# Deferred sum splits, a fifth pair of split weights, and seven products that grow in two PSUM tiles

## The chip, the cores and the metric

One core of one Trainium2 chip runs the whole program. The time is the device time of one execution in microseconds (us). TensorE (PE) multiplies, VectorE (DVE), ScalarE (ACT) and GpSimd (POOL) work elementwise, and SyncE (SP) issues the loads. Each engine works through its own list of instructions in the order in which the program was written or scheduled; an instruction that waits for another engine holds up all behind it.

## The reference

One step of a decoder layer over 1024 prompt tokens and 8 × 4 sample tokens, model width 1024. A mixing layer (windowed attention beside trailing-mean pooling) is followed by the part that this change touches, a feed-forward layer with 2816 hidden channels, and by an input per layer:

```python
f = _rms(x, n_ffn_pre)
f = (jax.nn.silu(f @ w_gate) * (f @ w_up)) @ w_down
x = x + _rms(f, n_ffn_post)
x = x + jax.nn.sigmoid(x @ w_ple_gate) * (p @ w_ple)
```

All is float32, to float32's accuracy.

## The kernel before

**Split products.** A float32 operand is split by `split` into a high part, cast on ACT (L164), and a low part, the rest, subtracted on DVE (L165). A product is three matmuls: high × high, high × low, low × high. All matmuls are issued from line 126; the tokens are the moving operand, 352 at a time, since the 1056 tokens form three groups `g` of 352.

**Weights.** Raw weights of 512 KB are loaded by SP into `wr` (`W_RAW` buffers), and split into `wh` and `wl` (`W_PAIRS` pairs, which also hold the sums `sh`, `sl`). `need(k)` makes all items up to `LOOK` = 4 ahead of the one wanted, in the order of `ITEMS`.

**Seven products.** For token groups 0 and 1 the gate and up product of one chunk of 128 channels is made with seven half-sized products instead of eight. The gate weight `wg` and the up weight `wu` give P1 and P2 and T4 (`p4`) by their quarters; four more products, S1 to S4, use sums and differences of quarters of both. POOL makes these in place in the raw buffers with four instructions (`w_sums`, L990), and then ACT and DVE split the two results into `sh` and `sl`. The token side (`B11`, `T1` and so on) was made once before. Each product (12 matmuls) has a PSUM tile of its own (`bank`, eight in turn); DVE adds them up from there (L1024), silu of the gate part is on ACT (L1036, L1067), and the two products of gate and up, one for each of the two token groups, go into `hid` with a split of their own (`hid_put`). Group 2 is multiplied directly (24 matmuls for gate, 24 for up).

**The walk.** There are 11 slabs of two chunks. `WALK` takes slabs 0 to 4 for group 2 alone (while other work still runs), slabs 5 to 10 for all three groups, and slabs 0 to 4 again for groups 0 and 1. The last five are called slabs 1 to 5 in what follows. In each, for chunk pair i = 0: P1, P2, then `pending()`, which is the down products of the slab before (six matmuls for each of 8 columns and each group; the high and low parts of `hid` for two chunks; DVE adds the result into `o`, L1087), then p4, S2, S3, S1, S4. "The downs of slab 2" are those that run inside slab 2. For pair i = 1 there are no downs: p4 and the S products follow P1 and P2. In the slabs with group 2, p4 stands between S3 and S1.

**Beside it.** When group 2 is finished (downs of slab 1), `ple_steps` follow in pieces: the norm factor is spread over the partitions by small matmuls, DVE multiplies `o` with it from a PSUM tile (L1115) and adds it to `x` (L1119).

Of the kernel before, what the change touches and what calls it, by code (L numbers as in the profile page):

```python
# [12 lines left out]
AF = mybir.ActivationFunctionType  # L13
ALU = mybir.AluOpType
# [33 lines left out]
UEXT = PST + DSEQ  # L48
ULEN = UPRE + SEQ + NDEC * UEXT

W_PAIRS = 4
W_RAW = 3


WARM = 8
# [6 lines left out]
def trunk_kernel(  # L62
# [31 lines left out]
    nc = tc.nc  # L94
    te, ve, se, ge = nc.tensor, nc.vector, nc.scalar, nc.gpsimd
# [28 lines left out]
    def mm(*args, **kw):  # L124

        ins = te.matmul(*args, **kw)  # L126
# [36 lines left out]
    def split(hi, lo, src):  # L163
        fix(se.copy(hi, src))  # L164
        fix(ve.tensor_tensor(lo, src, hi.bitcast(F32), op=ALU.subtract))  # L165
# [3 lines left out]
    def w_load(j):  # L169
        if j >= len(plan) or j in raws:  # L170
            return
        src, shape = plan[j]
        t = wpool.tile(shape, F32, tag="wr", bufs=W_RAW, name=nm("wr"))
        nc.sync.dma_start(t, src)
        raws[j] = t

    def w_tile(shape, s):
        return wpool.tile(shape, F32R, tag="wp", bufs=2 * W_PAIRS, name=nm(s))

    def w_split(j):  # L180
        if j >= len(plan) or j in pairs:
            return
        w_load(j)
        shape = plan[j][1]
        hi, lo = w_tile(shape, "wh"), w_tile(shape, "wl")
        split(hi, lo, raws[j])
        pairs[j] = (hi, lo)

    lazy = [False]

    def weights(j, ahead=W_PAIRS - 1):
        for i in range(j, j + (0 if lazy[0] else ahead) + 1):
            w_split(i)
            w_load(i + 1)
        return pairs[j]
# [19 lines left out]
    WALK += [(s, (0, 1)) for s in range(AHEAD)]  # L215
    ITEMS = []

    def item(kind, *js):
        ITEMS.append((kind, js))
        return len(ITEMS) - 1  # L220

    def direct_item(src, shape):
        return item("direct", add_plan(src, shape))

    WGU, WD = [], []
    for s, gs in WALK:
        pairs_of = []
        for i in range(SLAB):
            c = SLAB * s + i
            jg = direct_item(w_gu[c, 0], [P, KC, P])  # L230
            if 0 not in gs:
                ju = direct_item(w_gu[c, 1], [P, KC, P])
            if i == 0 and WD:
                last_s = WALK[len(WD) - 1][0]
                WD[-1] = [direct_item(w_dn[last_s, j], [P, SLAB, 512]) for j in range(2)]
            if 0 in gs:
                ju = direct_item(w_gu[c, 1], [P, KC, P])
            js = item("sums", jg, ju) if 0 in gs else None
            pairs_of.append((jg, ju, js))
        WGU.append(pairs_of)  # L240
        WD.append(None)
# [20 lines left out]
    made = {}  # L262

    def need(k, ahead=LOOK):

        for i in range(len(made), min(k + ahead + 1, len(ITEMS))):
            kind, js = ITEMS[i]
            if kind == "direct":
                w_split(js[0])
                made[i] = pairs[js[0]]  # L270
            else:
                made[i] = w_sums(*(raws[ITEMS[j][1][0]] for j in js))
            for kind, js in ITEMS[i + 1 : i + 3]:
                if kind == "direct":
                    w_load(js[0])
        return made[k]

    def gemm(ps, ops, start=True, stop=True):

        last = len(ops) - 1  # L280
        for i, (wh, wl, xh, xl) in enumerate(ops):
            mm(ps, wh, xh, start=start and i == 0, stop=False)
            mm(ps, wh, xl, start=False, stop=False)
            mm(ps, wl, xh, start=False, stop=stop and i == last)

    def ops8(w, xs):

# [53 lines left out]
    def load(dst, src):  # L341
        tc.keep_in_program_order(nc.sync.dma_start(dst, src))  # L342
# [92 lines left out]
    n = 4 * NDEC * PST  # L435
# [145 lines left out]
    for c in range(4):  # L581
        n = NDEC * DSEQ
# [356 lines left out]
    f7 = {}  # L939
# [37 lines left out]
    def hid_put(g, slot, ht):  # L977
        split(new_hid[g][:, slot, :], new_hid[g][:, SLAB + slot, :], ht)

    def w_sums(a1, a2):  # L980


        a11, a12, a21, a22 = a1[:, 0:4, :], a1[:, 4:8, :], a2[:, 0:4, :], a2[:, 4:8, :]
        for out, a, b, op in (
            (a22, a21, a22, ALU.add),
            (a21, a11, a21, ALU.subtract),
            (a11, a22, a11, ALU.subtract),
            (a12, a12, a11, ALU.subtract),
        ):
            ge.tensor_tensor(out, a, b, op=op)  # L990
        two = []
        for src in (a1, a2):
# [4 lines left out]
        return {"S2": quarter(s24, 0), "S4": quarter(s24, 1), "S3": quarter(s31, 0), "S1": quarter(s31, 1)}  # L997

    def ops4(w, x):

        return [(w[0][:, k, :], w[1][:, k, :], x[0][:, k, :], x[1][:, k, :]) for k in range(4)]

    def quarter(w, h):
        return tuple(t[:, 4 * h : 4 * h + 4, :] for t in w)

    def gate_up(items, slot, gs, pending):

        ig, iu, is_ = items
        n = N

        def product(w, x):
            ps = bank()
            gemm(ps[:, :n], ops4(w, x))
# [9 lines left out]
        def add(out, a, ps):  # L1023
            ve.tensor_tensor(out, a, ps, op=ALU.add)  # L1024

        wg = need(ig)
        if 0 in gs:
            p1 = tmp(n, "p1")
            se.copy(p1, product(quarter(wg, 0), f7["B11"]))
        if 2 in gs:  # L1030
            sl = tmp(n, "sl")
            se.activation(sl, direct(wg), AF.Silu)
        if 0 in gs:
            c11 = tmp(n, "c11")
            add(c11, p1, product(quarter(wg, 1), f7["B21"]))
# [4 lines left out]
        if 2 in gs:  # L1040
            ve.tensor_tensor(sl, sl, direct(wu), op=ALU.mult)
        for g in gs:
            if slot == 0:
                new_hid[g] = half(g, F32R, "hid")
        if 2 in gs:
            hid_put(2, slot, sl)
        if pending and 0 not in gs:
            pending()
        if 0 not in gs:
            return  # L1050
        if 2 not in gs:
            p4 = product(quarter(wu, 1), f7["T4"])
        s = need(is_)
        add(p1, p1, product(s["S2"], f7["T2"]))
        u3 = tmp(n, "u3")
        add(u3, p1, product(s["S3"], f7["T3"]))
        c21 = tmp(n, "c21")
        if 2 in gs:
            p4 = product(quarter(wu, 1), f7["T4"])
        add(c21, u3, p4)  # L1060
        ve.tensor_tensor(c21, c21, c11, op=ALU.mult)
        hid_put(0, slot, c21)
        p5 = product(s["S1"], f7["T1"])
        add(u3, u3, p5)
        add(p1, p1, p5)
        add(p1, p1, product(s["S4"], f7["B22"]))
        se.activation(p1, p1, AF.Silu)  # L1067
        ve.tensor_tensor(u3, u3, p1, op=ALU.mult)
        hid_put(1, slot, u3)

    os_ = [None] * G

# [204 lines left out]
```

## Time and profile before

| what | value |
|---|---|
| time, median of 3 runs | 1118.11 us (1117.52 to 1119.99) |
| the profiled execution, its own time | 1118.37 us |
| its span, first to last instruction | 1116.6 us |
| mean granted TensorE clock | 0.998 |
| busy, ACT | 440.0 us, 39% |
| DMA moved | 99.54 MB, 89 GB/s |

The span is that of the instructions; the execution is 1.8 us longer. Times in the timelines count from the span's start. The feed-forward part runs from about 219 to 1112 us.

### The profile page before, as it was taken

Reading aid. Unit: us, or ns where it says so; the run is one execution under the profiler, and the core shown is the slowest. Engines: PE = TensorE matmul, PEld = TensorE weight load, DVE = VectorE, ACT = ScalarE, POOL = GpSimd, SP = SyncE. Lnnn points to the kernel's source line nnn. Section 1 sums busy time; section 2 is a strip of 40 time slices with the busy share of each in tenths; the row PEclk is TensorE's granted clock in tenths of the full one; section 3 lists DMA queues with packets and bytes.
Section 4 is the critical chain, followed back from the end, with each engine's and each line's share of the span. In section 5 each row is a group of like instructions: output and inputs, shape, how many; then the busy total and the mean of one; then the engine's idle time right before and its main releaser. Section 6 shows DMA issues by size and latency. Waiting matters only on the chain.

```text
span 1116.6 us, 17703 instructions
## 1 busy us (share of the span) xinstructions
PE 1106.5 (99%) x7171; PEld 1089.6 (98%) x7171; DVE 748.3 (67%) x1241; ACT 440.0 (39%) x779; POOL 179.4 (16%) x152
## 2 busy tenths in 40 slices
PE   8999999999999999999999999999999999999998
PEld 8999988899999999999999999999999999999998
DVE  6667478886979955255564555547887877789532
ACT  8323276664645523331222313123424334365220
POOL 0045032200000131011111102112132123100000
PEclk9999999999999999999999999999999999999999
DMA  8121311542543212121120202122112222336211
GB/s 289 56 71 38 122 43 38 194 157 85 203 166 129 99 38 76 39 76 39 38 60 17 78 36 76 38 100 79 57 58 83 70 76 80 124 133 222 85 58 39
DMA packets 35217, 99.54 MB, mean 89 GB/s; under 512 B 4132, under 2 KB 14660, under 8 KB 35136
## 3 DMA queue, kind: packets, MB, share of 16 engines
q1 hardware_dynamic: 33808, 96.65, 25.5%
q10 hardware_dynamic: 1328, 1.77, 0.5%
q8 instruction: 56, 0.92, 0.3%
q14 instruction: 25, 0.20, 0.1%
HBM read 88.30 MB, written 10.11 MB: 88 GB/s over the span
## 4 chain that ended last, share of the span: by engine, by line
PE 93%; DVE 3%; DMA 1%; issue 1%; POOL 1%; ACT 1%; SPq 0%; DVEq 0%; POOLq 0%
PE b L126 92%; PE b L120 1%; DMA xr<-in_x_dram 1%; DVE wl L165 1%; POOL wr L990 0%; SPq L342 0%; DVE h L368 0%; DVE o L1115 0%; DVE x L1119 0%; DVE mx L628 0%; DVE a L736 0%; DVE p L1024 0%; DVE hid L165 0%; ACT h L366 0%; ACT xr L377 0%
## 5 line engine op out<-in xcount | busy, mean ns | idle before, releaser
L126 PE MATMUL b<-fh,wh 128*128 128x352 f32 x808 | 260.7, 323 | 0.0
L126 PE MATMUL b<-fh,wl 128*128 128x352 f32 x808 | 259.3, 321 | 0.0
L126 PE MATMUL b<-fl,wh 128*128 128x352 f32 x808 | 259.0, 321 | 0.0
L126 PE MATMUL b<-hid,wh 128*128 128x352 f32 x1056 | 252.5, 322 | 1.8 <-DVE o L1115 1.2
L164 ACT CAST wh<-wr 128x1024 fp32r<-128x1024 f32 (+1 forms) x139 | 143.0, 1031 | 248.9 <-PE b L126 205.6
L165 DVE TENSOR_TENSOR wl<-wr,wh 128x1024 fp32r<-128x1024 f32 (+1 forms) x139 | 170.5, 1229 | 57.9 <-ACT wh L164 53.9
L126 PEld LDWEIGHTS b<-hid,wh 128*128 128x128 f32 x1056 | 182.3, 188 | 2.6 <-issue 1.5
L126 PE MATMUL b<-hid,wl 128*128 128x352 f32 x528 | 169.0, 320 | 0.0
L990 POOL TENSOR_TENSOR wr<-wr 128x512 f32<-128x512 f32 x44 | 63.4, 1441 | 623.0 <-DVE wl L165 621.3
L126 PEld LDWEIGHTS b<-fl,wh 128*128 128x128 f32 x808 | 151.9, 188 | 0.0
L126 PEld LDWEIGHTS b<-fh,wl 128*128 128x128 f32 x808 | 151.8, 188 | 0.0
L126 PEld LDWEIGHTS b<-fh,wh 128*128 128x128 f32 x808 | 151.6, 188 | 0.0
L1087 DVE TENSOR_TENSOR o<-o,b 128x352 f32<-128x352 f32 x240 | 114.9, 516 | 29.3 <-PE b L126 29.3
L126 PE MATMUL b<-fh,sh 128*128 128x352 f32 x352 | 113.6, 323 | 0.0
L126 PE MATMUL b<-fl,sh 128*128 128x352 f32 x352 | 112.7, 320 | 0.0
L126 PE MATMUL b<-fh,sl 128*128 128x352 f32 x352 | 112.7, 320 | 0.0
L126 PE MATMUL b<-h,wh 128*128 128x352 f32 x480 | 105.5, 325 | 0.9 <-ACT h L366 0.6
L165 DVE TENSOR_TENSOR sl<-wr,sh 128x1024 fp32r<-128x1024 f32 x44 | 53.8, 1222 | 75.5 <-ACT sh L164 75.5
L126 PEld LDWEIGHTS b<-hid,wl 128*128 128x128 f32 x528 | 98.9, 187 | 0.0
L164 ACT CAST sh<-wr 128x1024 fp32r<-128x1024 f32 x44 | 45.7, 1047 | 130.9 <-POOL wr L990 91.2
L126 PEld LDWEIGHTS b<-h,wh 128*128 128x128 f32 x480 | 81.9, 189 | 2.2 <-DVE h L368 1.2
L126 PE MATMUL b<-h,wl 128*128 128x352 f32 x240 | 66.3, 326 | 0.0
(150 smaller groups left out, 1591.0 us busy)
## 6 DMA issues: line engine op xcount, KB each, us to landing
wr<-in_w_gu_dram SPq DMA_DIRECT2D x64, 512.0 KB, 3.3
wr<-in_w_dn_dram SPq DMA_DIRECT2D x32, 512.0 KB, 3.3
wr<-in_w_pg_dram SPq DMA_DIRECT2D x14, 512.0 KB, 3.6
x<-in_x_dram SPq DMA_DIRECT2D x6, 704.0 KB, 7.1
x1d<-x SPq DMA_DIRECT2D x6, 704.0 KB, 3.5
x<-x1d SPq DMA_DIRECT2D x6, 704.0 KB, 6.7
out_y_dram<-yo SPq DMA_DIRECT2D x24, 176.0 KB, 1.9
wr<-in_w_out_b_dram SPq DMA_DIRECT2D x8, 512.0 KB, 3.3
```

Of the source, the lines that this page charges most:

```text
L120: ins = te.transpose(out, src, ident)
L126: ins = te.matmul(*args, **kw)
L164: fix(se.copy(hi, src))
L165: fix(ve.tensor_tensor(lo, src, hi.bitcast(F32), op=ALU.subtract))
L990: ge.tensor_tensor(out, a, b, op=op)
L1087: ve.tensor_tensor(o, o, v, op=ALU.add)
```

## The change

Four things change.

1. `W_PAIRS` goes from 4 to 5 and `W_RAW` from 3 to 4. The room comes from a smaller scratch for dynamic DMA.
2. `w_sums` only adds on POOL (now L1005). The split of the sums is `split_sums`. For pair i = 1 of a slab it follows at once as before; for pair i = 0 (`BEHIND`) it follows after the first half of the down products of each slab (`split_unsplit`), or when the sum is first wanted.
3. The seven products grow in two tiles. P1 opens `row`; S2·T2, S3·T3 and, with group 2, T4 are added onto it by PE. S1·T1 opens `col`; S4·B22 is added onto it. What is wanted of a tile in between is copied out by ACT (`copied`, L1050: p1, u2, p5 and, without group 2, u3), and PE adds on only after the copy has read the tile. The products' order becomes S2, S1, S3, S4.
4. Without group 2, p4 keeps a tile of its own, ahead of S2. With group 2 the up part of group 2 goes behind S4, and T4 is last.

The program has as many matmuls as before, 78 DVE instructions fewer and 54 ACT instructions more; POOL and SP have the same number.

```diff
-W_PAIRS = 4
-W_RAW = 3
+W_PAIRS = 5
+W_RAW = 4
...
+            if js and i == 0:
+                BEHIND.add(js)
...
                 made[i] = w_sums(*(raws[ITEMS[j][1][0]] for j in js))
+                if i in BEHIND:
+                    unsplit.append(i)
+                else:
+                    split_sums(i)
...
+        if k in unsplit:
+            split_unsplit()
         return made[k]
...
+    def split_unsplit():
+        while unsplit:
+            split_sums(unsplit.pop())
...
+        def copied(ps, s):
+            out = tmp(n, s)
+            se.copy(out, ps)
+            return out
+
+        third = 2 in gs
         wg = need(ig)
         if 0 in gs:
-            p1 = tmp(n, "p1")
-            se.copy(p1, product(quarter(wg, 0), f7["B11"]))
+            row = bank()
+            p1 = copied(product(quarter(wg, 0), f7["B11"], row), "p1")
...
-        add(p1, p1, product(s["S2"], f7["T2"]))
-        u3 = tmp(n, "u3")
-        add(u3, p1, product(s["S3"], f7["T3"]))
-        c21 = tmp(n, "c21")
-        if 2 in gs:
-            p4 = product(quarter(wu, 1), f7["T4"])
-        add(c21, u3, p4)
-        ve.tensor_tensor(c21, c21, c11, op=ALU.mult)
-        hid_put(0, slot, c21)
-        p5 = product(s["S1"], f7["T1"])
-        add(u3, u3, p5)
-        add(p1, p1, p5)
-        add(p1, p1, product(s["S4"], f7["B22"]))
-        se.activation(p1, p1, AF.Silu)
-        ve.tensor_tensor(u3, u3, p1, op=ALU.mult)
-        hid_put(1, slot, u3)
+        u2 = copied(product(s["S2"], f7["T2"], row, False), "u2")
+        p5 = copied(product(s["S1"], f7["T1"], col), "p5")
+        p7 = product(s["S3"], f7["T3"], row, False)
+        if not third:
+            u3 = copied(p7, "u3")
+        u1 = add(p5, p7, "u1")
+        if not third:
+            ve.tensor_tensor(u3, u3, p4, op=ALU.add)
+            ve.tensor_tensor(u3, u3, c11, op=ALU.mult)
+            hid_put(0, slot, u3)
+        c12 = add(u2, product(s["S4"], f7["B22"], col, False), "c12")
+        se.activation(c12, c12, AF.Silu)
+        ve.tensor_tensor(u1, u1, c12, op=ALU.mult)
+        hid_put(1, slot, u1)
+        if third:
+            third_up()
+            ve.tensor_tensor(c11, c11, product(quarter(wu, 1), f7["T4"], row, False), op=ALU.mult)
+            hid_put(0, slot, c11)
...
                     if g in gs:
                         (last_down if g == 2 and s == NSLAB - 1 else down)(n, m, g)
+            split_unsplit()
```

The following three places show the order on an engine. The first is ACT in slab 5, pair i = 0, from the last down product on. Before:

```order
L164 CAST wh1392_8955<-wr1374_8837 128x1024
L164 CAST wh1402_9023<-wr1385_8918 128x1024
L164 CAST hid1418_9107<-c211427_9159 128x352
L164 CAST sh1413_9097<-wr1374_8837 128x1024
L164 CAST sh1415_9101<-wr1385_8918 128x1024
L1067 ACTIVATE p11386_8920<-p11386_8920 128x352
L1029 COPY p11433_9203<-b1434_9204 128x352
```

and now:

```order
L164 CAST wh1378_8975<-wr1357_8862 128x1024
L1050 COPY u21401_9095<-b1358_8864 128x352
L164 CAST sh1389_9049<-wr1349_8776 128x1024
L1050 COPY p51402_9109<-b1399_9067 128x352
L164 CAST sh1391_9053<-wr1357_8862 128x1024
L1050 COPY u31403_9123<-b1358_8864 128x352
```

Here `wh` is the up weight's cast, which waits for the last down product; the two `sh` casts are of pair 1's sums, which POOL makes. Before, a silu and the next P1's copy followed them; now the copies of u2, p5 and u3 stand around them, the p5 copy behind the first `sh`. The same order stands in slabs 2 to 4.

The second place is ACT in slab 1, pair i = 0, also from the cast that follows the last down product. Before:

```order
L164 CAST wh1164_7589<-wr1147_7462 128x1024
L164 CAST wh1182_7700<-wr1159_7556 128x1024
L304 ACT_TABLE_LOAD
L304 ACTIVATE sd1218_7874<-b1217_7869,c8_86 88x4
L164 CAST sh1201_7818<-wr1147_7462 128x1024
L164 CAST hid1206_7828<-c211224_7900 128x352
L164 CAST sh1203_7822<-wr1159_7556 128x1024
L1029 COPY p11230_7944<-b1231_7945 128x352
```

and now:

```order
L164 CAST wh1158_7652<-wr1131_7500 128x1024
L319 ACT_TABLE_LOAD
L319 ACTIVATE sd1194_7826<-b1193_7821,c8_86 88x4
L164 CAST sh1177_7770<-wr1124_7390 128x1024
L1050 COPY u21198_7836<-b1132_7502 128x352
L1050 COPY p51199_7850<-b1187_7788 128x352
L164 CAST sh1179_7774<-wr1131_7500 128x1024
L1050 COPY u31200_7864<-b1132_7502 128x352
```

The cast of the first sum (`sh1177`) now stands ahead of both copies, u2 and p5.

The third place is DVE ahead of the downs of slab 2, whose first instructions want `hid1182` (`hid1206` before). Before:

```order
L1061 TENSOR_TENSOR c211244_8033<-c211244_8033,c111232_7959 128x352
L1024 TENSOR_TENSOR u31242_8018<-u31242_8018,b1245_8038 128x352
L165 TENSOR_TENSOR hid1206_7828<-c211244_8033,hid1206_7828 128x352
L1024 TENSOR_TENSOR p11230_7944<-p11230_7944,b1245_8038 128x352
L165 TENSOR_TENSOR wl1235_7976<-wr1211_7847,wh1234_7975 128x1024
L1024 TENSOR_TENSOR p11230_7944<-p11230_7944,b1246_8053 128x352
L165 TENSOR_TENSOR wl1238_7993<-wr1229_7942,wh1237_7992 128x1024
L1115 TENSOR_TENSOR o534_3284<-o534_3284,b1241_8011 128x1408
L1068 TENSOR_TENSOR u31242_8018<-u31242_8018,p11230_7944 128x352
L1119 SCALAR_TENSOR_TENSOR x21215_7865<-o534_3284,c1_72,x21215_7865 128x352 x2
L165 TENSOR_TENSOR hid1207_7829<-u31242_8018,hid1207_7829 128x352
L1024 TENSOR_TENSOR c111254_8100<-p11252_8085,b1255_8101 128x352
```

and now:

```order
L165 TENSOR_TENSOR wl1213_7932<-wr1205_7894,wh1212_7931 128x1024
L1147 TENSOR_TENSOR o534_3284<-o534_3284,b1217_7963 128x1408
L1045 TENSOR_TENSOR u11221_7999<-p51219_7983,b1206_7896 128x352
L1151 SCALAR_TENSOR_TENSOR x21191_7817<-o534_3284,c1_72,x21191_7817 128x352 x2
L1091 TENSOR_TENSOR u31220_7997<-u31220_7997,b1216_7938 128x352
L1045 TENSOR_TENSOR c121222_8017<-u21218_7969,b1215_7937 128x352
L1092 TENSOR_TENSOR u31220_7997<-u31220_7997,c111209_7924 128x352
L1045 TENSOR_TENSOR c111227_8059<-p11225_8042,b1226_8044 128x352
L1096 TENSOR_TENSOR u11221_7999<-u11221_7999,c121222_8017 128x352
L165 TENSOR_TENSOR hid1182_7780<-u31220_7997,hid1182_7780 128x352
```

`o534` times the norm factor (L1115, now L1147) and the two additions into `x` (L1119, now L1151) stood behind the low half of the first part of hid; now they stand ahead of all that makes it: u3 plus p4 (L1091), times c11 (L1092), and the subtraction (L165).

More of the change, by code (lines that the diff above doesn't have):

```diff
@@ L216, in trunk_kernel @@
     ITEMS = []
+    BEHIND = set()
     def item(kind, *js):
@@ L260, in trunk_kernel @@
         WPE[1][m] = wp, direct_item(w_pg[m], [P, KC, P])
-    made = {}
+    made, unsplit = {}, []
     def need(k, ahead=LOOK):
@@ L275, in need, with gemm @@
                     w_load(js[0])
+        if k in unsplit:
+            split_unsplit()
         return made[k]
-    def gemm(ps, ops, start=True, stop=True):
+    def split_unsplit():
+        while unsplit:
+            split_sums(unsplit.pop())
+    def gemm(ps, ops, start=True, stop=True, onto=False):
         last = len(ops) - 1
         for i, (wh, wl, xh, xl) in enumerate(ops):
-            mm(ps, wh, xh, start=start and i == 0, stop=False)
-            mm(ps, wh, xl, start=False, stop=False)
-            mm(ps, wl, xh, start=False, stop=stop and i == last)
+            mm(ps, wh, xh, start=start and i == 0, stop=False, skip_group_check=onto)
+            mm(ps, wh, xl, start=False, stop=False, skip_group_check=onto)
+            mm(ps, wl, xh, start=False, stop=stop and i == last, skip_group_check=onto)
     def ops8(w, xs):
@@ L990, in w_sums, with split_sums @@
             ge.tensor_tensor(out, a, b, op=op)
+        return a1, a2
+    def split_sums(i):
         two = []
-        for src in (a1, a2):
+        for src in made[i]:
             hl = w_tile([P, KC, P], "sh"), w_tile([P, KC, P], "sl")
@@ L996, in w_sums @@
         (s24, s31) = two
-        return {"S2": quarter(s24, 0), "S4": quarter(s24, 1), "S3": quarter(s31, 0), "S1": quarter(s31, 1)}
+        made[i] = {"S2": quarter(s24, 0), "S4": quarter(s24, 1), "S3": quarter(s31, 0), "S1": quarter(s31, 1)}
     def ops4(w, x):
@@ L1009, in gate_up, with product @@
         n = N
-        def product(w, x):
-            ps = bank()
-            gemm(ps[:, :n], ops4(w, x))
+        def product(w, x, ps=None, start=True):
+            onto = ps is not None
+            ps = ps if onto else bank()
+            gemm(ps[:, :n], ops4(w, x), start, onto=onto)
             turn(12)
@@ L1021, in direct, with add @@
             return ps[:, :n]
-        def add(out, a, ps):
+        def add(a, ps, s):
+            out = tmp(n, s)
             ve.tensor_tensor(out, a, ps, op=ALU.add)
+            return out
+        def copied(ps, s):
+            out = tmp(n, s)
+            se.copy(out, ps)
+            return out
+        third = 2 in gs
         wg = need(ig)
         if 0 in gs:
-            p1 = tmp(n, "p1")
-            se.copy(p1, product(quarter(wg, 0), f7["B11"]))
-        if 2 in gs:
+            row = bank()
+            p1 = copied(product(quarter(wg, 0), f7["B11"], row), "p1")
+        if third:
             sl = tmp(n, "sl")
@@ L1033, in gate_up @@
         if 0 in gs:
-            c11 = tmp(n, "c11")
-            add(c11, p1, product(quarter(wg, 1), f7["B21"]))
+            c11 = add(p1, product(quarter(wg, 1), f7["B21"]), "c11")
             se.activation(c11, c11, AF.Silu)
@@ L1039, in gate_up @@
         wu = need(iu)
-        if 2 in gs:
-            ve.tensor_tensor(sl, sl, direct(wu), op=ALU.mult)
         for g in gs:
@@ L1044, in gate_up, with third_up @@
                 new_hid[g] = half(g, F32R, "hid")
-        if 2 in gs:
+        def third_up():
+            ve.tensor_tensor(sl, sl, direct(wu), op=ALU.mult)
             hid_put(2, slot, sl)
-        if pending and 0 not in gs:
-            pending()
         if 0 not in gs:
+            third_up()
+            if pending:
+                pending()
             return
-        if 2 not in gs:
+        s = need(is_)
+        col = bank()
+        if not third:
             p4 = product(quarter(wu, 1), f7["T4"])
-        s = need(is_)
-        add(p1, p1, product(s["S2"], f7["T2"]))
-        u3 = tmp(n, "u3")
-        add(u3, p1, product(s["S3"], f7["T3"]))
-        c21 = tmp(n, "c21")
-        if 2 in gs:
-            p4 = product(quarter(wu, 1), f7["T4"])
-        add(c21, u3, p4)
-        ve.tensor_tensor(c21, c21, c11, op=ALU.mult)
-        hid_put(0, slot, c21)
-        p5 = product(s["S1"], f7["T1"])
-        add(u3, u3, p5)
-        add(p1, p1, p5)
-        add(p1, p1, product(s["S4"], f7["B22"]))
-        se.activation(p1, p1, AF.Silu)
-        ve.tensor_tensor(u3, u3, p1, op=ALU.mult)
-        hid_put(1, slot, u3)
+        u2 = copied(product(s["S2"], f7["T2"], row, False), "u2")
[4 more added lines that the diff above has]
+        u1 = add(p5, p7, "u1")
+        if not third:
+            ve.tensor_tensor(u3, u3, p4, op=ALU.add)
[5 more added lines that the diff above has]
+        hid_put(1, slot, u1)
+        if third:
+            third_up()
+            ve.tensor_tensor(c11, c11, product(quarter(wu, 1), f7["T4"], row, False), op=ALU.mult)
+            hid_put(0, slot, c11)
     os_ = [None] * G
@@ L1252 @@
     from concourse.bass_utils import run_bass_kernel_spmd as _run
-    nc = _bacc.Bacc("TRN2", target_bir_lowering=False, num_devices=1)
+    nc = _bacc.Bacc("TRN2", target_bir_lowering=False, num_devices=1, dynamic_dma_scratch_size=1024)
     arrays, args = {}, []
```

## The prediction

> **What bounds the kernel now.** The page was read first (busy shares, chain), then the groups, the waits, and last the timelines of the stretches in which PE stood.
>
> ```profile
> span 1116.6 us, 17703 instructions
> ...
> PE 1106.5 (99%) x7171; PEld 1089.6 (98%) x7171; DVE 748.3 (67%) x1241; ACT 440.0 (39%) x779; POOL 179.4 (16%) x152
> ...
> PE 93%; DVE 3%; DMA 1%; issue 1%; POOL 1%; ACT 1%; SPq 0%; DVEq 0%; POOLq 0%
> ...
> L126 PE MATMUL b<-hid,wh 128*128 128x352 f32 x1056 | 252.5, 322 | 1.8 <-DVE o L1115 1.2
> ...
> L990 POOL TENSOR_TENSOR wr<-wr 128x512 f32<-128x512 f32 x44 | 63.4, 1441 | 623.0 <-DVE wl L165 621.3
> ```
>
> TensorE is the bound: 1106.5 of 1116.6 us, 93% of the chain. The whole idle time is 10.1 us, most of it in the first 28 us and after the last matmul. In the channel part the big idle sums stand on the other engines:
>
> ```profile
> POOL wr L990 <- DVE wl L165: 621.3, 22, 169.4
> ACT sh L164 <- POOL wr L990: 91.2, 22, 6.3
> ```
>
> POOL's sums start when a second weight has been split, and ACT's split of a sum waits up to 6.3 us for POOL. Today that wait costs nothing, since nothing that PE soon needs stands behind it on ACT. PE stands only here in this part, by its timeline:
>
> ```profile
> 816.62 0.32 PE L126 MATMUL b<-hid,wh 128*128 128x352 f32 x1
> 817.51 0.43 PE L126 MATMUL b<-hid,wh 128*128 128x352 f32 x1 [0.57 <-DVE hid L165]
> ...
> 863.71 0.32 PE L126 MATMUL b<-hid,wl 128*128 128x352 f32 x1
> 865.25 0.56 PE L126 MATMUL b<-hid,wh 128*128 128x352 f32 x2 [1.22 <-DVE o L1115]
> ```
>
> Matmuls start 0.159 us apart (next fence), so these lose 0.89 − 0.16 = 0.73 and 1.54 − 0.16 = 1.38 us, **2.11 us in all**. That is nearly all that the change could win there.
>
> **The model slab.** In the last five slabs a fixed pattern follows the down products. One of them, on PE, ACT, DVE and POOL:
>
> ```profile
> 955.90 0.32 PE L126 MATMUL b<-fh,wh 128*128 128x352 f32 x1
> 963.52 0.32 PE L126 MATMUL b<-fh,sh 128*128 128x352 f32 x1
> ...
> 955.98 1.05 ACT L164 CAST wh<-wr 128x1024 fp32r<-128x1024 f32 x1 [6.56 <-PE b L126]
> 966.17 2.00 ACT L164 CAST sh<-wr 128x1024 fp32r<-128x1024 f32 x2 [2.19 <-POOL wr L990]
> ...
> 957.07 1.22 DVE L165 TENSOR_TENSOR wl<-wr,wh 128x1024 fp32r<-128x1024 f32 x1 [0.45 <-ACT wh L164]
> 958.98 1.23 DVE L165 TENSOR_TENSOR wl<-wr,wh 128x1024 fp32r<-128x1024 f32 x1 [0.68 <-ACT wh L164]
> ...
> 960.33 1.29 POOL L990 TENSOR_TENSOR wr<-wr 128x512 f32<-128x512 f32 x1 [15.22 <-DVE wl L165]
> 964.69 1.45 POOL L990 TENSOR_TENSOR wr<-wr 128x512 f32<-128x512 f32 x1
> ```
>
> Call the start of p4's product T (955.90). Four products of 12 matmuls later it is 963.52, so a product takes 7.62 / 4 = 1.905 us and a matmul 0.159. The split chain: `wh` T+0.08 to T+1.13, `wl` to T+2.39; POOL starts 0.12 after the `wl` it waits for and takes 966.14 − 960.33 = 5.81 us for its four sums; ACT's split of a sum follows 0.03 later and takes 1.0 to 1.05.
>
> **Matmuls.** Their number and kinds stay, so PE's work is the same; only stalls count. 78 fewer DVE instructions win nothing where DVE isn't waited for (67% busy).
>
> **The copies (L1050).** One copy of a product:
>
> ```profile
> 938.99 0.45 ACT L1029 COPY p<-b 128x352 f32<-128x352 f32 x1 [0.36 <-PE b L126]
> ```
>
> 54 more on an engine that is 39% busy are hidden as work: 54 × 0.45 = 24 us. But PE now waits for them: a product may be added onto a tile only when the earlier value has been copied out. In the six slabs with the third group, both copies stand ahead of the splits that wait for POOL, and each is ready 0.5 us after its product with a whole product (1.9 us) between: cost 0. In the last five slabs it is otherwise, by ACT's order shown with the change.
>
> *S4 onto `col`, slabs 2 to 5.* ACT's order is `wh`, u2 copy, split of a sum (waits for POOL), p5 copy. POOL now waits for the first `wl`: it runs from T+2.39+0.12 = T+2.51 to T+8.32. The split starts at T+8.35, the p5 copy about 0.97 later and is done at T+9.77; PE follows at T+9.83. PE has p4, S2, S1 and S3 to do, so S4 was due at T+4×1.905 = T+7.62. **Stall 2.2 us, four times: +8.8.** From below: 0, if the copy were free of the split; from above 2.2 + 0.97, if both splits came first.
>
> *S3 onto `row`, slab 1.* Here the u2 copy itself stands behind the split. It is done at about T+9.8 and S3 starts at T+9.87. Due after p4, S2, four small matmuls and S1, T+5.7 + 0.4 or 0.5 = T+6.2: **+3.6**. p5's copy then follows at T+10.2, ahead of its S4.
>
> **Parts of hid, down products.** Before, the products' results went through DVE in pieces, and the first part of hid was ready long before the downs. Now its value needs S3 as well, after DVE's work. In slab 2, DVE's order puts the post-norm steps ahead (rows of before, same operations):
>
> ```profile
> 810.82 1.61 DVE L1115 TENSOR_TENSOR o<-o,b 128x1408 f32<-128x1408 f32 x1
> 812.35 0.52 DVE L1068 TENSOR_TENSOR u<-u,p 128x352 f32<-128x352 f32 x1
> 812.79 3.15 DVE L1119 SCALAR_TENSOR_TENSOR x<-o,c,x 128x352 f32<-128x352 f32 x2
> 815.85 1.60 DVE L165 TENSOR_TENSOR hid<-u,hid 128x352 fp32r<-128x352 f32 x1
> ...
> 812.41 3.14 POOL L990 TENSOR_TENSOR wr<-wr,wr 128x512 f32<-128x512 f32 x2
> 815.63 1.45 POOL L990 TENSOR_TENSOR wr<-wr 128x512 f32<-128x512 f32 x1
> ...
> L1119 DVE SCALAR_TENSOR_TENSOR x<-o,c,x 128x352 f32<-128x352 f32 x24 | 15.3, 664 | 0.0
> ```
>
> Beside POOL's sums two such steps take 3.15 us where the mean of one is 0.664, and they end 0.4 us after a POOL instruction has: 815.94 after 815.55, 817.45 after 817.08. POOL holds them up. With D the start of the downs, S3 ends three products earlier, at D−5.7. Then `wh` and `wl` (2.3 us) to D−3.4, POOL from D−3.3 to D+2.5, o·r to D−1.9, u1 to D−1.4, the two steps, each let in at a POOL end (D−0.4, D+1.05), to D+1.5; two adds and a product of 0.45 to 0.52 to D+2.9, ACT's cast of hid to D+3.5. PE wants the cast at its fourth matmul, D+0.48: 3.05 us late. The low half, three DVE instructions further, is 0.55 later still: **+3.6** (2.0 if the two steps ran at 0.664). The 0.73 of before in this place is gone.
>
> In the downs of slabs 3, 4 and 5 ACT casts hid's second part behind the split that waits for POOL (to D+2.5), and DVE has that sum's low half ahead of hid's:
>
> ```profile
> 861.27 1.05 ACT L164 CAST sh<-wr 128x1024 fp32r<-128x1024 f32 x1 [2.90 <-POOL wr L990]
> 862.35 1.23 DVE L165 TENSOR_TENSOR sl<-wr,sh 128x1024 fp32r<-128x1024 f32 x1 [3.71 <-ACT sh L164]
> ```
>
> Split to D+3.6, `sl` to D+4.83, hid's low half to D+5.35 with 0.52; PE wants it after four down groups and four matmuls, 28 × 0.159 = D+4.45. **+0.95, three times: +2.85.** (Ends: 0, and 2.0 if hid also waits a POOL sum.) The 1.38 of before goes, since o·r no longer stands behind that `sl` while a bank is wanted.
>
> **Later splitting, five pairs, four raw buffers.** These let weights be loaded and split earlier in the first part, whose idle is another wait's; I take 0, with ±1 us from the head and the tail.
>
> **TensorE's clock.** The head shows what a pause does:
>
> ```profile
> 21.56 0.81 PE L126 MATMUL b<-h,wl 128*128 128x352 f32 x4
> 23.70 0.79 PE L126 MATMUL b<-c,acc 128*88 128x1 f32 x8 [1.33 <-DVE acc L334]
> ...
> 24.30:27.80 3.50, 3.32 (x16) 2.90 (x15) 3.47 (x11) 3.43 (x6) 0.86 (x2) 0.65 0.06 19
> 27.80:31.00 3.20, 3.20 (x18) 3.11 (x19) 3.20 (x6) 2.41 (x5) 0.00 (x0) 0.84 0.00 0
> 862.00:866.00 4.00, 2.78 (x18) 2.52 (x17) 3.65 (x5) 1.37 (x2) 0.00 (x0) 1.00 0.31 109
> ```
>
> After 1.33 us of idle and tiny matmuls the granted clock (third number from the end) is 0.65 and 0.84 in the next two stretches: 3.50 × 0.35 + 3.20 × 0.16 = 1.7 us lost. After the 1.54 us pause at 863.7 it stayed 1.00. I count one drop, at the longest pause: **+1.7**. The Trainium skill, page "TensorE: Matmul & The Clock Gate", section "Why this matters for your kernels", warns of pauses of more than about 3 us between bursts, by which slab 1's pause and slab 2's would each drop the clock and the 2.2 us ones would not; that rule alone would make the sum 1.7 higher, and the head's drop after a shorter pause speaks against its bound.
>
> **Sum.** The profiled execution took 1118.37 us (span 1116.6 and 1.8 around it), 0.26 above the median of 1118.11. 1118.37 + 8.8 + 3.6 + 3.6 + 2.85 − 2.11 + 1.7 = 1136.8; less 0.26, **1136.5 us**.
>
> **Rivals.**
> - *Only the S4 stalls are real* (hid is ready in time, slab 1's u2 copy too): 1118.11 + 8.8 − 2.11 = 1124.8. For it: DVE is 67% busy and has 78 instructions fewer; against: the stalled casts stand in a fixed order.
> - *The clock falls at all six pauses over 2 us*, five more drops: 1136.5 + 5 × 1.7 = 1145. For it: the head's pause of 1.33 us; against: 863.7.
> - *The other side, faster.* If with five pairs the split that starts POOL's sums comes before the last down groups, at least 2.2 us earlier, every wait for POOL is over when its copy is due, the pauses at 816 and 863 go, and the time is 1118.11 − 2.11 = 1116.0. Against: that cast takes a buffer that the last down product still reads.
> - *Nothing happens.* The waits are all covered and two pauses of the old size stay somewhere: 1118.1.
>
> **How the numbers follow.** Forecast 0.50, only S4 0.17, clock 0.20, faster 0.05, nothing 0.05, longer than all these 0.03. Range 1124 to 1146: both slower rivals and the ends of the hid and copy terms. A measurement of this kernel tells about 0.2% (2.2 us) from no change: faster 0.05, same 0.05, slower 0.90.
>
> **What would show it.** In the profile after: PE idle some 27 us instead of 10; four idle rows of about 2.2 us at a matmul with `sh`, released by ACT's copy L1050; one of 3.6 us in slab 1; pauses released by hid in the downs of slabs 2 to 5; ACT's copy waiting behind a cast that POOL releases; no row of PE waiting for o. I am wrong if the copies are seen ahead of those casts, if POOL's sums end before T+5.5, or if the clock stays at 1.00 after the longest pause (then 1.7 less).

## The result and the profile after

| | before | after |
|---|---|---|
| median | 1118.89 us (5 runs, 1117.52 to 1119.99) | 1137.58 us (5 runs, 1135.93 to 1138.15) |
| ratio | | 1.0167, 95% interval 1.0156 to 1.0178 |
| span of the profiled execution | 1116.6 us | 1136.0 us |

The page after, the lines that answer to those of before: busy shares, and the two groups of matmuls before which PE now stands (the last column is the idle time ahead of them and what ended most of it).

```profile
PE 1111.2 (98%) x7171; PEld 1092.6 (96%) x7171; DVE 732.1 (64%) x1163; ACT 463.7 (41%) x833; POOL 188.8 (17%) x152
...
L126 PE MATMUL b<-hid,wh 128*128 128x352 f32 x1056 | 254.9, 324 | 7.2 <-DVE hid L165 4.5
...
L126 PE MATMUL b<-fh,sh 128*128 128x352 f32 x352 | 114.8, 326 | 8.8 <-ACT p L1050 5.9
```

PE has as many matmuls as before and is idle 1136.0 − 1111.2 = 24.8 us instead of 10.1. Its waits after, by what ended them (total, times, longest):

```profile
PE b L126 <- ACT p L1050: 5.9, 4, 1.5
PE b L126 <- DVE hid L165: 4.5, 4, 1.4
PE b L126 <- ACT u L1050: 2.9, 1, 2.9
PE b L126 <- ACT hid L164: 2.7, 1, 2.7
```

By releaser these are the pauses that the prediction named: p5's copy four times, u2's once, hid four times from DVE and once from ACT. Three of DVE's four stand at another place than it said, as the section on slabs 3 to 5 shows. One pause of the first kind, on PE, ACT and POOL (timeline, start and duration; in brackets the idle time and what ended it):

```profile
935.56 0.32 PE L126 MATMUL b<-fh,sl 128*128 128x352 f32 x1
937.39 0.43 PE L126 MATMUL b<-fh,sh 128*128 128x352 f32 x1 [1.51 <-ACT p L1050]
...
930.52 1.29 POOL L1005 TENSOR_TENSOR wr<-wr 128x512 f32<-128x512 f32 x1 [16.17 <-DVE wl L165]
934.62 1.29 POOL L1005 TENSOR_TENSOR wr<-wr 128x512 f32<-128x512 f32 x1
...
935.94 1.04 ACT L164 CAST sh<-wr 128x1024 fp32r<-128x1024 f32 x1 [3.38 <-POOL wr L1005]
936.89 0.45 ACT L1050 COPY p<-b 128x352 f32<-128x352 f32 x1
```

POOL ends at 935.91, the cast begins 0.03 later, the copy 0.95 after that, and PE follows at 937.39. The p product that is copied was long done; only the cast ahead of the copy waits for POOL.

From the matmuls' starts in the trace, each pause less the usual 0.159:

| term | predicted | after |
|---|---|---|
| S4, slabs 2 to 5 | 4 × 2.2 = 8.8 | 1.55 + 1.67 + 1.67 + 1.63 = 6.5, and 0.4 for slower matmuls just behind |
| S3, slab 1 | 3.6 | 3.1 |
| hid, slab 2 | 3.6 | 2.88 + 0.63 = 3.5 |
| hid, slabs 3 to 5 | 3 × 0.95 = 2.85 | 1.55 + 1.55 + 1.51 = 4.6, and 0.6 for slower matmuls |
| clock | one drop, 1.7 | two drops, 1.4 + 1.6 = 3.0 |
| pauses of before | −2.1 | −2.1 |
| sum | 18.4 | 19.6 (the spans differ by 19.4) |

### The profile page after: what moved, and what is told of

It reads as the page before. It is cut to its first block, busy times and chain, and to the rows that moved or that the text cites. A ratio compares the mean times of both kernels' runs of the same rounds, so it can differ in the third digit from the quotient of the medians.

```text
span 1136.0 us, 17639 instructions
## 1 busy us (share of the span) xinstructions
PE 1111.2 (98%) x7171; PEld 1092.6 (96%) x7171; DVE 732.1 (64%) x1163; ACT 463.7 (41%) x833; POOL 188.8 (17%) x152
## 4 chain that ended last, share of the span: by engine, by line
PE 42%; issue 36%; POOL 11%; DMA 5%; DVE 3%; ACT 2%; SPq 0%; POOLq 0%; ACTq 0%; DVEq 0%
PE b L126 41%; POOL wr L1005 11%; DMA wr<-in_w_gu_dram 4%; DVE sl L165 2%; ACT sh L164 1%; DMA xr<-in_x_dram 1%; PE b L120 1%; DMA a<-in_dmask_dram 1%; SPq L357 0%; DVE mx L643 0%; DVE a L751 0%; DVE c L1045 0%; DVE wl L165 0%; ACT wh L164 0%; ACT h L381 0%
## 5 line engine op out<-in xcount | busy, mean ns | idle before, releaser
L165 DVE TENSOR_TENSOR wl<-wr,wh 128x1024 fp32r<-128x1024 f32 (+1 forms) x139 | 174.6, 1257 | 76.9 <-ACT wh L164 72.7
L1005 POOL TENSOR_TENSOR wr<-wr 128x512 f32<-128x512 f32 x44 | 65.5, 1489 | 631.2 <-DVE wl L165 629.5
L1119 DVE TENSOR_TENSOR o<-o,b 128x352 f32<-128x352 f32 x240 | 118.1, 517 | 44.9 <-PE b L126 44.7
L165 DVE TENSOR_TENSOR sl<-wr,sh 128x1024 fp32r<-128x1024 f32 x44 | 53.8, 1223 | 60.4 <-ACT sh L164 52.1
L126 PEld LDWEIGHTS b<-fh,sh 128*128 128x128 f32 x352 | 66.5, 189 | 10.2 <-ACT p L1050 7.0
```

What stands on the lines that cost most here:

```text
L1119: ve.tensor_tensor(o, o, v, op=ALU.add)
```

## Experiments

The ratios are against the kernel before as it ran beside each group of runs: 1117.85 us for `e1` to `e4`, 1118.06 for `e5` to `e8`, 1118.28 for `e9` to `e11`. Beside the change it was 1118.89, so times of different groups compare to about 1 us only.

### The copies on ACT: does PE wait for the order there?

`e1_copies_first` moves the split of pair 1's sums in the last five slabs behind S3's copies (`late` is a list like `unsplit`).

```diff
+            if js and i and s < AHEAD:
+                LATE.add(js)
...
+                elif i in LATE:
+                    late.append(i)
...
+        while late and slot == 0:
+            split_sums(late.pop())
         u1 = add(p5, p7, "u1")
```

> The change, but the sums of pair 1 in the last five slabs are split only after S3, so that on ACT both copies (u2, p5) stand ahead of the first split that waits for POOL. Theory of the prediction (the copies wait in ACT's queue behind that split): the four pauses before S4 (1.55 to 1.67 us, with a slower matmul after each 6.9 in all), the pause of 3.1 us before S3 in slab 1 and the clock drop after it (1.4) go, the pauses at hid stay: 1137.6 - 11.4 = about 1126. Rival (the copies are late for another reason, or PE waits for the bank and not for the copy): the pauses before S3 and S4 stay, 1137 to 1138.

Measured: 1126.14 us, ratio 1.0075 (1.0060 to 1.0090). The group of matmuls that S3 and S4 begin with, in this run:

```profile
L126 PE MATMUL b<-fh,sh 128*128 128x352 f32 x352 | 113.6, 323 | 0.0
```

No idle time is left there. The time fell by 11.4 us, as the terms gave, or by 10.4 when each run is taken against the kernel before beside it (18.7 us over it for the change, 8.3 here). Part of the fit is luck: the drop of the clock in slab 2 lasted for 18 matmuls here and not 9, which took back 1.1 us. The order on ACT, and not the accumulation as such, is what S3 and S4 wait for.

### What holds hid up in slabs 3 to 5

The trace after shows this pause at another place than predicted: at the first down group, for the low half of hid's *first* part, not at the fifth group for its second. PE, DVE and POOL there:

```profile
911.56 0.32 PE L126 MATMUL b<-hid,wh 128*128 128x352 f32 x1
913.26 0.43 PE L126 MATMUL b<-hid,wh 128*128 128x352 f32 x1 [1.38 <-DVE hid L165]
...
909.39 2.31 DVE L165 TENSOR_TENSOR wl<-wr,wh 128x1024 fp32r<-128x1024 f32 x1
911.62 1.58 DVE L165 TENSOR_TENSOR hid<-u,hid 128x352 fp32r<-128x352 f32 x1
...
909.16 3.66 POOL L1005 TENSOR_TENSOR wr<-wr,wr 128x512 f32<-128x512 f32 x2
912.90 1.45 POOL L1005 TENSOR_TENSOR wr<-wr 128x512 f32<-128x512 f32 x1
```

Beside POOL's sums DVE's `wl` takes 2.31 us, where the mean is 1.22 to 1.26, and hid's low half 1.58 instead of 0.52. The low half ends at 913.20, 0.38 behind POOL's instruction that ended at 912.82. POOL was held up too: the second of the two sums in its row of 3.66 us took 2.13, where 1.29 is usual, and its four sums together 6.56 instead of the 5.39 at 930.52.

Two runs tell this hold from ACT's order. `e2_split_at_once` takes the deferral away (`BEHIND` stays empty), which puts hid's second cast ahead of the split on ACT and leaves POOL where it is:

```diff
-            if js and i == 0:
-                BEHIND.add(js)
```

> The change without the deferral: the sums of pair 0 are split as soon as they are made, all else as in the change. In slabs 3 to 5 ACT then casts hid's second part ahead of the split that waits for POOL. Theory of the prediction for these pauses (hid waits on ACT behind the split): they go, 5 us less there. Rival (seen in the trace after: POOL's sums hold up DVE's own instructions, the low half of the up weight and of hid): they stay at 1.5 us or more each. In slab 2 the cast of hid's first part now stands behind two splits that wait for POOL, so its pause grows from 3.5 to about 5. Rival's time: about 1139; the theory's: about 1134.

Measured: 1137.6 us, ratio 1.0173 (1.0158 to 1.0188). The pauses in slabs 3 to 5 are still there, but shorter (0.87 instead of 1.55):

```profile
866.34 0.32 PE L126 MATMUL b<-hid,wh 128*128 128x352 f32 x1
867.36 0.43 PE L126 MATMUL b<-hid,wh 128*128 128x352 f32 x1 [0.70 <-DVE hid L165]
```

In slab 2 PE stands for 5.1 us, as expected about 5, since hid's first cast is there behind two splits. So neither theory alone had it: the deferral changed the order around the hold, and POOL's hold remained without it. The equal time is a balance of the two, and no sign that the deferral does nothing.

`e5_sums_after_hid` makes POOL wait until hid is complete; POOL's order is pinned to the written one:

```diff
+    seen = const([P, 1], dt=F32R)
...
-            ge.tensor_tensor(out, a, b, op=op)
+            tc.keep_in_program_order(ge.tensor_tensor(out, a, b, op=op))
...
+        if not third and slot == 1:
+            tc.keep_in_program_order(ge.tensor_copy(seen, new_hid[1][:, SLAB + 1, 0:1]))
```

> The change, but in the last five slabs POOL makes pair 0's sums only after the low half of hid's second part is written (a copy of one column from it stands ahead of the sums on POOL). Theory (two holds together: DVE's own instructions beside POOL's sums, and hid's cast and low half behind the split that waits for POOL): the pauses at hid in slabs 3 to 5 go (1.55 + 0.2 each, 5.2 in all), and in slab 2 the two norm steps run at their free speed, so that pause falls from 3.5 to about 2 and no clock drop of 1.6 follows: 1137.6 - 5.2 - 3.1 = about 1129. The pauses before S3 and S4 stay. Rival (hid is late by its own chain, u3 copy, two DVE steps, cast, low half): all the pauses at hid stay, 1137.

Measured: 1133.22 us, ratio 1.0133 (1.0119 to 1.0147). The pauses in slabs 3 to 5 are gone. In slab 2 two smaller ones stand:

```profile
819.97 0.32 PE L126 MATMUL b<-hid,wl 128*128 128x352 f32 x1
821.01 0.43 PE L126 MATMUL b<-hid,wh 128*128 128x352 f32 x1 [0.72 <-ACT hid L165]
821.79 0.43 PE L126 MATMUL b<-hid,wh 128*128 128x352 f32 x1 [0.36 <-DVE hid L166]
```

That is 0.88 + 0.63 = 1.5 us instead of 3.5, and no drop of the clock after it. In slab 4 DVE has the same order as in the change, and its `wl` took 1.22 us again and hid's low half 0.52. So POOL's sums are what held hid's first part up; for the second part, the split that waits for them moved as well. The time is 4 us over the expected 1129, though: 3.1 of it lie in the slabs *before* those that were edited, which the section on all three edits together takes up, and 0.6 at a bank that DVE frees late in the downs of slab 2.

### The norm steps ahead of hid in slab 2

`e6_norm_later` moves them 60 matmuls on:

```diff
+        if g == 2:
+            yield 60, 0
         for h in range(2):
             yh, xh = os_[g][h], x2[g][h]
```

> The change, but the post-norm steps of group 2 (o times the factor and what follows) are put 60 matmuls later, so that on DVE they no longer stand ahead of hid's first part in slab 2. Theory: slab 2's pause of 3.5 us falls to that of slabs 3 to 5 (1.7) and its clock drop (1.6, with a slower start 0.3) goes: 1137.6 - 3.7 = about 1134. Rival (POOL's sums and the ACT order alone make that pause): 1137 to 1138.

Measured: 1135.91 us, ratio 1.0162 (1.0147 to 1.0178). Slab 2's pause fell from 3.5 to 1.55 us, that of its neighbours, without a drop of the clock. Some of it came back where the moved steps now stand: 0.35 us at a bank in slab 4's downs, and 2.0 instead of 1.63 before slab 5's S4. The gain against the change, 1.7 us (0.8 when each is taken against the kernel before beside it), is at most half of what was expected and no larger than the spread of its runs (1134.9 to 1137.3); the pause itself is the evidence.

### Pairs, or tiles

`e3_four_pairs` sets `W_PAIRS` to 4 and `W_RAW` to 3 and keeps the rest; `e4_own_tiles` keeps five pairs, four raw buffers and the deferral, and takes the whole of `gate_up` from the kernel before.

```diff
-W_PAIRS = 5
-W_RAW = 4
+W_PAIRS = 4
+W_RAW = 3
```

> The change with W_PAIRS 4 and W_RAW 3, as before it; the two tiles and the deferral stay. With one pair less, the split of pair 1's sums finds no room before S3 has read its weights, so ACT has both copies ahead of it. Theory (the order on ACT, made by the fifth pair, is what costs): no pause before S3 or S4, no pause of 1.5 us at hid's low half in slabs 3 to 5 (half a us at most); in slab 2 some 4 us and one clock drop stay, since DVE's order is the same: 1118.4 - 2.1 + 4.1 + 1.5 + 1.5 = about 1123. Rival (the two tiles themselves cost, whatever the number of pairs): about as the change, 1135 to 1138.

Measured: 1136.34 us, ratio 1.0165 (1.0150 to 1.0181). The theory's 1123 was wrong. ACT's order did become as said, and no pause before S4 is released by p5's copy, but hid's chain got later instead. In slab 2 (PE, then DVE):

```profile
819.01 0.42 PE L126 MATMUL b<-hid,wh 128*128 128x352 f32 x1 [0.90 <-ACT hid L164]
822.64 0.66 PE L126 MATMUL b<-hid,wh 128*128 128x352 f32 x1 [3.20 <-DVE hid L165]
...
817.99 3.09 DVE L1151 SCALAR_TENSOR_TENSOR x<-o,c,x 128x352 f32<-128x352 f32 x2
821.01 1.58 DVE L165 TENSOR_TENSOR hid<-u,hid 128x352 fp32r<-128x352 f32 x1
```

4.5 us in all, with 19 matmuls at the lower clock behind it; in slabs 3 to 5 hid's second part is 1.4 us late each, and S3 waits for u2's copy up to 0.85. Not all of its time is a wait of this kind: in the slabs with group 2, from 338 to 787 us, PE issued 2798 matmuls where it issued 2827 before, some 4.6 us. About 1.5 of that are 12 short gaps, and the rest is a slower stream (0.160 us apart, not 0.159), which the section on all three edits takes up. The fifth pair is thus not the cause alone: with fewer pairs the same two tiles wait at other places.

> The change's five pairs, four raw buffers and deferral, but the seven products as before it, each in its own tile and added up on DVE. Theory (only the two tiles make PE wait for ACT's copies): no pause before S3 and S4, and hid's first part is ready ahead of the downs as before: 1117 to 1120. Rival (five pairs and deferral cost by themselves, by POOL's earlier start beside DVE's work): 1122 or more, with pauses at hid.

Measured: 1121.35 us, ratio 1.0030 (1.0019 to 1.0042), about 1 over the range of the theory and under that of its rival. S3 and S4 have no pause. The excess is hid beside POOL's earlier sums (0.4 to 0.8 us in five places), a bank that DVE frees late in the downs of slabs 3 and 4 (1.6 and 0.6 us), and again a slower stream: 529 matmuls from 910 to 995 us, where before had 537, 1.3 us. The two pauses of before, 2.1 us, are gone. So five pairs and the deferral together cost 3.5 us here without the tiles (1121.35 against 1117.85), and the two tiles on top of them 15 to 16 (1137.58 against 1121.35, or 18.7 over the kernel before against 3.5).

### From which pause the clock falls

`e8_longer1` writes the first high half of pair 1's sums twice (the same values), so that p5's copy stands behind two casts.

```diff
...
+            if i in LATE and src is made[i][0]:
+                for _ in range(1):
+                    fix(se.copy(hl[0], src))
             split(*hl, src)
```

> The change, with the first high half of pair 1's sums cast twice on ACT in the last five slabs (the second writes the same again), so that each pause before S4 grows by 0.95 to about 2.6, and that before S3 in slab 1 to 4.1. It asks from which pause TensorE's clock falls. If only pauses of 3 us or more drop it: 5 x 0.95 more and one drop at S3 as before, 1142.4. If a pause of 2.6 does too: up to four drops of 1.5 more, 1144 to 1148.

Measured: 1146.22 us (two runs), ratio 1.0250 (1.0231 to 1.0269). The four pauses before S4 are 2.6 to 2.75 us, as meant; S3's stayed at 3.1, since u2's copy stands between the two casts on ACT. The stretches behind four of its pauses, and behind two of `e2_split_at_once` (start and end, length, busy time of PE and of the others, then the granted clock, the DMA share and GB/s):

```profile
820.70:824.00 3.30, 3.30 (x20) 3.30 (x21) 3.30 (x7) 0.98 (x2) 0.00 (x0) 1.00 0.02 5
846.00:849.40 3.40, 3.40 (x12) 3.40 (x13) 3.00 (x4) 1.25 (x2) 0.00 (x0) 0.51 0.39 149
942.60:946.00 3.40, 3.40 (x21) 3.40 (x22) 3.24 (x5) 2.27 (x3) 0.00 (x0) 1.00 0.43 146
989.30:992.70 3.40, 3.37 (x12) 3.37 (x13) 3.02 (x4) 1.28 (x2) 0.00 (x0) 0.52 0.37 125
```

```profile
792.80:796.20 3.40, 3.38 (x21) 3.39 (x22) 1.11 (x2) 1.65 (x3) 0.00 (x0) 1.00 0.44 141
820.00:825.40 5.40, 5.40 (x18) 5.13 (x19) 4.69 (x9) 0.68 (x2) 0.00 (x0) 0.51 0.54 196
```

Three of the four pauses of 2.6 to 2.75 us dropped the clock and one (before 942.6) did not; behind S3's 3.1 us it fell in the changed kernel, 1.3 us late in this run, and not at all in `e2_split_at_once`; behind slab 2's 2.9 + 0.6 it fell in the changed kernel, and not in this run (the row from 820.70). The pauses of 1.5 to 1.7 us never dropped it in any run. So no fixed length between 2.6 and 3.3 decides.

The trace's record of the granted clock shows what does. In this run the clock falls at 794.86, 846.06, 893.85 and 989.42, each time for 3.41 us, and these moments lie 15, 14 and 28 times 3.413 us apart. So the clock is set for fixed windows of 3.41 us, and what counts is how long PE is idle within one of them. PE in two such windows at the second of the four pauses (before 894.4) and in three at the third (before 942.6) (length and busy time, then the granted clock, the DMA share and GB/s):

```profile
890.43:893.85 3.42, 1.46 (x10) 1.00 0.00 0
893.85:897.26 3.41, 2.89 (x10) 0.50 0.30 90
...
938.21:941.62 3.41, 1.89 (x12) 1.00 0.00 0
941.62:945.04 3.42, 2.46 (x15) 1.00 0.17 43
945.04:948.45 3.41, 3.41 (x23) 1.00 0.76 267
```

The second pause left PE idle for 3.42 − 1.46 = 1.96 us of one window, and the next window ran at half the clock. The third, just as long, lay across the edge of two windows, with 1.52 us idle in one and 0.96 in the other, and the clock stayed. S3's pause in `e2_split_at_once` was split in the same way (1.28 and 1.66). In the 13 traces, from 330 us on, half the clock followed each of the 11 windows at full clock with 1.96 us or more of idle time, and none of the 44 with 0.8 to 1.84. The loss behind a drop was 8 to 19 matmuls at 0.293 us instead of 0.159. The Trainium skill, "TensorE: Matmul & The Clock Gate", section "What's actually happening", describes a free-running window of some 3.4 us, and the windows of 3.41 us in these traces agree with that. The same page of the Trainium skill advises, in "Why this matters for your kernels", to avoid pauses above about 3 us; for these runs that is too mild, since 2.6 us was enough three times.

### All three together, and a surprise

`e7_all_three` joins the edits of the first, third and fourth of these runs.

> The change with all three moved: sums of pair 1 split after S3, sums of pair 0 made after hid, norm steps 60 matmuls later. If the terms add up, all of 3.1 + 1.4 + 6.9 (copies), 5.2 (hid, slabs 3 to 5) and 5.4 (slab 2 with its clock drop) go: 1137.6 - 22 = 1115.6, that is 2 us faster than the kernel before, since its two pauses of 0.73 and 1.38 are gone too. Rival (what is moved collides elsewhere, as the norm steps did with a bank before): 1118 to 1121.

Measured: 1121.78 us, ratio 1.0036 (1.0023 to 1.0048): 6 us over what the terms gave. The pauses are gone but for 0.26 and twice 0.33 us at banks and 1.1 before an S3 in slab 5. Half of the 6 us is no pause: from 338 to 787 us, where PE has no pause either in the kernel before or in this run, PE issued fewer matmuls in the same 449 us. Before, and in this run:

```profile
338.00:787.00 449.00, 449.00 (x2827) 1.00 0.19 63
```

```profile
338.00:787.00 449.00, 449.00 (x2809) 1.00 0.18 62
```

That is 449/2827 = 0.1588 against 449/2809 = 0.1598 us from matmul to matmul, at the same granted clock. The run with the sums after hid shows it as well, and both have one more small tile (`seen`) ahead of the weight buffers; `e3_four_pairs`, which shows it without that tile, has fewer buffers. Two runs test the tile:

```diff
-    seen = const([P, 1], dt=F32R)
...
-            ... ge.tensor_copy(seen, new_hid[1][:, SLAB + 1, 0:1]) ...
+            ... ge.tensor_copy(ones[:, 64:65], new_hid[1][:, SLAB + 1, 0:1].bitcast(F32)) ...
```

> The same as the run with all three moved, but POOL's one-column copy goes into a column of a tile that is there already, so that no tile of four bytes per partition is added. In that run and in the one with the sums after hid the matmuls of the slabs with group 2 (338 to 787 us) stood 0.160 us apart and not 0.159, 3.1 us in all, with no pause between them. If the added tile (it shifts the tiles behind it) does that: 1121.8 - 3.1 = 1118.7. If POOL's fixed order does it: 1121.8 as there.

and, in the kernel before:

```diff
     ge.memset(epst, EPS)
+    spare = const([P, 1])
+    ge.memset(spare, 0.0)
```

> The kernel before with one unused tile of 128 x 1 float32 ahead of the weight buffers, and nothing else. If the place of the tiles sets how fast matmuls follow each other: the matmuls from 338 to 787 us take about 3 us longer than before, 1121 in all. If not: 1118.1.

Measured: 1118.89 us, ratio 1.0002 (0.9993 to 1.0011), and 1121.16 us, ratio 1.0031 (1.0019 to 1.0043). Without the tile the stream is back, with it even the kernel before loses 3 us. The stretch of the latter:

```profile
338.00:787.00 449.00, 449.00 (x2808) 1.00 0.18 62
```

So 3 of the 4 us that `e5_sums_after_hid` was over, and 3 of the 6 here, were the place of the tiles, shown by both runs. For `e3_four_pairs` and `e4_own_tiles`, whose buffers also lie elsewhere, that is likely and not shown. Which tile matters, and how, wasn't tried.

### Can the change's idea be had without its cost?

`e9_no_new_tile` is the change with its three orders put right, and equals the kernel before within about 1 us. With PE as the bound, fewer DVE instructions and five pairs won nothing. The two old pauses were all that there was to win, and new ones (1.1 before an S3, 0.3 at a bank) took most of that back. `e11_before_norm_later` aims at the old pauses alone, with the edit of `e6_norm_later` in the kernel before:

> The kernel before with the post-norm steps of group 2 put 60 matmuls later, and nothing of the change. Its two pauses in this part (0.73 at hid, 1.38 at the bank that o times the factor frees) both come from these steps. If both go: 1118.1 - 2.1 = 1116.0. If the steps meet another bank or another wait: 1117.5 to 1119.

Measured: 1118.44 us, ratio 1.0000 (0.9991 to 1.0009). The pauses at 816 and 863 went, and the steps met another bank, as the rival said:

```profile
904.45 0.32 PE L126 MATMUL b<-hid,wl 128*128 128x352 f32 x1
905.27 0.58 PE L126 MATMUL b<-hid,wh 128*128 128x352 f32 x2 [0.50 <-DVE o L1087]
```

With 0.66 there and 0.26 more near 995, 2.1 − 0.9 = 1.2 us should have stayed as a gain. The runs don't show it: the interval ends at 0.9991, a gain of 1.0 us. In the profiled execution the matmuls ahead of the edit stood 0.8 us later than before (790.02 against 789.25 for the same one), so that a gain of this size may be hidden by the spread of the first part; it stays open. None of the edited kernels was faster than the kernel before.

## Why the prediction was right, point by point

- **PE is the bound and the change adds only pauses.** Right: the busy time rose from 1106.5 to 1111.2 us, most of it slower matmuls behind pauses (3.0 + 0.4 + 0.6 in the table), and the idle time by 14.7 us. No pause stands in the slabs with group 2, as was said.
- **S4 in slabs 2 to 5, S3 in slab 1.** Right in mechanism and place, shown by `e1_copies_first`. The sizes were 6.9 and 3.1 instead of 8.8 and 3.6. For S4 most of the difference is that POOL's four sums took 935.91 − 930.52 = 5.39 us and not the 5.81 of before. For S3 they took 5.60, and S3 was due 0.2 us later than counted.
- **hid in slab 2.** Right: 3.5 for 3.6. `e6_norm_later` shows the part of the norm steps, `e5_sums_after_hid` that of POOL's hold on them.
- **hid in slabs 3 to 5.** This step failed, in place and in size. The prediction said that "ACT casts hid's second part behind the split that waits for POOL" and took 0.95 at the fifth down group (its own times give 5.35 − 4.45 = 0.90). That order does stand in the trace after: in slab 4 the cast begins at 915.33, behind the split's at 914.38. But PE had been held for 1.55 by then, at the first group, where POOL's sums held DVE's `wl` and the low half of hid's first part, and the second part came only 0.09 to 0.11 late. The prediction had quoted this hold for slab 2's steps; in slabs 3 to 5 it stood only at the end of the range (2.0 "if hid also waits a POOL sum").
- **The clock.** One drop of 1.7 was counted; there were two, of 1.4 and 1.6, both behind pauses of about 3 us. The prediction had weighed a second drop and set the drop in the head, after 1.33 us of idle, against it. The head's stretch held tiny matmuls too, so it was no measure of a pause among full ones, where windows with up to 1.84 us of idle time kept the clock. The rival that all six pauses drop it was wrong: the 1.5 to 1.7 us ones did not.
- **Later splitting and five pairs at 0.** Not quite: `e4_own_tiles` puts them at 3.5 us in a kernel without the tiles, 1.3 of it the slower stream. In the change what they cost in waits lies within the terms above (the hold on hid), so that it isn't missing from the sum.
- **The other rivals** (only S4, 1124.8; faster, 1116.0; nothing, 1118.1): the pauses at hid and before S3 exclude the first, and the cast that starts POOL's sums did wait for the last down product, as was argued against the second.

The terms that were too high (2.4 in S3 and S4) and those that were too low (2.4 in hid, 1.3 in the clock) nearly cancel. The total, 1137.6 against 1136.5, is better than its parts, and that is luck.

## What to carry to other kernels

When products are made to grow in one PSUM tile, the copy in between becomes something that PE waits for: look at what stands ahead of that copy on its engine, above all work that waits for a third engine, before counting the additions that are saved. With PE at 99%, fewer instructions on the other engines won nothing here, and nearly every new wait of PE counted in full. Compare a kernel with an added tile only after its matmuls' spacing far from the edit has been checked.

## What the runs showed of the hardware that was not expected

- One tile of 128 × 1 float32 ahead of the weight buffers made 2,800 matmuls of 128 × 352 follow each other at 0.1599 instead of 0.1588 us, 3.0 us in all, at a granted clock of 1.00 (`e10_before_and_tile`).
- POOL's sums held up some of DVE's instructions and not others: beside them hid's low half took 1.58 us instead of 0.52 and `wl` 2.31 instead of 1.22, while additions with a PSUM operand kept their 0.51 to 0.52. DVE held POOL up as well: a sum took 2.13 instead of 1.29.
- The granted clock was set for fixed windows of 3.41 us. Half the clock followed each of 11 windows in which PE was idle for 1.96 us or more, and none of 44 with 0.8 to 1.84 us. A pause of 2.6 us could thus drop the clock (three times) or not (once), by where it lay.
